# A list scheduler that ranks the operations that read PSUM first, in a two-layer hybrid mixer

## The chip, the cores and the metric

The kernel runs on one core of a Trainium2 chip. The core has a matrix engine (TensorE, PE in the rows; its weight loads are a row of their own, PEld), a vector engine (VectorE, DVE), a scalar engine (ScalarE, ACT), GpSimd (POOL) and a queue of transfers issued by SyncE (SP). TensorE writes its results into PSUM; VectorE and ScalarE read them there and put them into SBUF, which is called an eviction here. The metric is the time of the program on the device in microseconds (us).

## The reference

Two layers of a transformer-like mixer. Four token mixers share one input projection; each result is gated, projected up, merged under a sigmoid gate, and projected out. 512 latent tokens and 256 context tokens; the context stream is updated in the first layer only. All numbers are fp32.

```python
def reference(x, c, ctx, c_ctx, norm_gain, w_mod, b_mod, w_in, ...):
    xc = ctx
    for l in range(DEPTH):                       # 2 layers, D_MODEL 1024, 512 latent and 256 context tokens
        need_ctx = l < DEPTH - 1
        shift, scale, gate = jnp.split((silu_c @ w_mod[l] + b_mod[l])[:, None, :], 3, axis=-1)
        shift_c, scale_c, gate_c = jnp.split(silu_cc @ w_mod[l] + b_mod[l], 3)
        h = rmsnorm(x, norm_gain[l]) * (1.0 + scale) + shift
        hc = rmsnorm(xc, norm_gain[l]) * (1.0 + scale_c) + shift_c
        za, zb, zh, zf, zg = jnp.split(h @ w_in[l], SPLIT_IDX, axis=-1)      # 15 blocks of 256 columns
        zc = hc @ (w_in[l] if need_ctx else w_in[l][:, :SPLIT_IDX[2]])
        ya, yca = mixer_diff_attn(za, ...)       # softmax attention, differential, rotary
        yb, ycb = mixer_neigh_attn(zb, ...)      # windowed softmax attention with a bias
        yh, ych = mixer_hgrn2(zh, ...)           # gated linear recurrence, both directions
        yf = fourier_mix(zf)                     # 2-D DFT
        x = x + gate * merge_branches(h, (ya, yb, yh, yf), zg, w_up[l], w_merge[l], w_out[l])
        if need_ctx:
            xc = xc + gate_c * merge_branches(hc, (yca, ycb, ych, ycf), zc_parts[4], ...)
    return x

def merge_branches(h, ys, g, w_up_l, w_merge_l, w_out_l):
    gs = jnp.split(g, N_BRANCH, axis=-1)
    acc = None
    for i in range(N_BRANCH):
        branch = (ys[i] * jax.nn.silu(gs[i])) @ w_up_l[i]
        term = jax.nn.sigmoid(h @ w_merge_l[i]) * branch
        acc = term if acc is None else acc + term
    return acc @ w_out_l
```

## The kernel before

**How the work is tiled.** Every large product is done on tiles of 128 rows by 256 to 512 columns. To keep fp32 precision each factor is split into a high part and a rest, and each product is three matmuls: high by high, high by rest, rest by high. For the weights, blocks `wraw` of 128x1024 are fetched by SyncE's queue; ScalarE writes the high part `wh` and VectorE the rest `wl`, in halves of 128x512 (`split`, L488; class `Weights`, L492). There are two buffers for `wraw` and four each for `wh` and `wl`. For the activations the split pair is `h_hi` and `h_lo`.

**PSUM.** It is divided into three pools (L369 to L371): three buffers of 128x512 named `psg` for the large products and many small ones, one buffer `pst`, and two of 128x1024 named `psw`. A tile must be evicted before its buffer takes the next one. `psg` of the merge is read by a tanh on ScalarE into `mth` (`merge`, L1481); `psg` of a modulation or gate is made by `spread` (L617: eight products with a block of 32 columns, `psg<-u,cst`) and copied by ScalarE into `mrow` (`mod_rows`, L633).

**The layer boundary.** At the end of the first layer the output projection of each 128 tokens is multiplied by the gate on VectorE (`gu<-psg,u`), added to the stream (`u<-u,gu`), squared and summed. From the sums VectorE computes a reciprocal square root in a chain of small steps (`rsqrt`, L472; tiles `sm`), scales an identity matrix by it (`u<-kc,sm`), and TensorE multiplies the stream by that diagonal, which transposes and normalises it at once (`place`, L760; `psw<-u,u`). Two of the four 128x128 pieces of each such `psw` are evicted by ScalarE, two by VectorE (`u<-psw,modc`); then the result is split into `h_hi` and `h_lo`.

**What sets the order.** No instruction is issued where it is written. Each call is noted as an operation (`Program.record`, L199); neighbouring matmuls into one tile form one operation, which `mm3` (L580) cuts after every four products of three. Transfers are operations too. When all are known, `Program.order` (L255) builds the order that all engines follow: over and over it looks at the operations that are ready on each engine, computes from a table of costs when each could start (its producers' ends, its engine, a free buffer), and takes the one with the smallest pair of start time and rank (L289 and L303). Rank decides only between operations that could start at the same moment on one engine, or between engines. Rank is an operation's place in the program as written, less `ahead`: the fetches and splits of weights have `ahead` 400 (`AHEAD`, L165, set at L504 and L515), all others 0. Only operations up to 300 places beyond the oldest that isn't done are looked at (`WINDOW`, L286). `emit` then writes the instructions in this order, all at one line (L353), so that the rows of the profile are told apart by their tiles. On the chip each engine runs its own list strictly in that order.

**The stages.** In each layer the projections and the mixers are laid one over the other: first the Fourier, recurrence and differential-attention projections, then four merges (Fourier, recurrence, differential attention, neighbourhood attention), then the output projection and, after the first layer, the boundary. The first layer takes about 0 to 890 us, the second the rest.

Of the kernel before, what the change touches and what calls it, by code (L numbers as in the profile page):

```python
# [135 lines left out]
def _overlap(a, b):  # L136
    if a[0] >= b[1] or b[0] >= a[1]:
        return False
    return any(x0 < y1 and y0 < x1 for x0, x1 in a[2] for y0, y1 in b[2])


def _covers(a, b):
    return a[0] <= b[0] and a[1] >= b[1] and all(any(x0 <= y0 and y1 <= x1 for x0, x1 in a[2]) for y0, y1 in b[2])
# [20 lines left out]
WINDOW = 300  # L164
AHEAD = 400  # L165
BEHIND = 0
ATOM = 4
LAT = {"tensor": 0.2, "vector": 0.13, "scalar": 0.15, "gpsimd": 0.13}


class Program:
# [27 lines left out]
    def record(self, engine, method, args, kw):  # L199
        writes = [v for v in [args[0], kw.get("accum_out")] if isinstance(v, View)]  # L200
        reads = [v for v in list(args[1:]) + [v for k, v in kw.items() if k != "accum_out"] if isinstance(v, View)]
        dma = method == "dma_start"
        last = self.last
        if engine == "tensor" and last is not None and last.engine == "tensor" and last.tiles[0] is args[0].tile:
            op = last
        else:
            op = Op(len(self.ops), engine)
            op.rank -= self.ahead
            self.ops.append(op)
        self.last = op  # L210
        op.calls.append((engine, method, args, kw))
        for v in writes + reads:
            if v.tile not in op.tiles:
                op.tiles.append(v.tile)
                v.tile.touch += 1
        for v, w in [(v, False) for v in reads] + [(v, True) for v in writes]:
            r = v.region()
            log = v.tile.log
            for q, x, xw in log:
                if (w or xw) and x is not op and _overlap(r, q):  # L220
                    op.preds.add(x)
            if w:
                log[:] = [e for e in log if not _covers(r, e[0])]
            log.append((r, op, w))
        op.cost += self.price(engine, method, args, kw)
        op.latency = 2.0 if dma else LAT[engine]
        if dma:
            op.transfer = math.prod(args[0].shape) * 4 / 3e5
# [129 lines left out]
def tile_hybrid_mixers(ctx, tc, io, out, dump=None):  # L358
# [28 lines left out]
    def psg():  # L387
        return pg.tile([P, 512], F32, tag="g", name=nm("psg"))
# [7 lines left out]
    def act(out, in_, func=AF.Copy, **kw):  # L396
        nc.scalar.activation(out, in_, func, **kw)
# [181 lines left out]

    def mm3(ps, pairs, atom=ATOM):  # L580
        n = len(pairs)
        nc.ahead = -BEHIND
        for k, (sh, sl, mh, ml) in enumerate(pairs):
            if k % atom == 0:
                nc.cut()
            mm(ps, sh, mh, k == 0, False)
            mm(ps, sh, ml, False, False)
            mm(ps, sl, mh, False, k == n - 1)
        nc.ahead = 0

    def gemm_a(wh, wl, cs, n0, n1, ps=None, atom=ATOM):
        ps = (psg() if ps is None else ps)[:, 0:n1 - n0]
        mm3(ps, [(wh[k][:, cs], wl[k][:, cs], hi_t[:, k, n0:n1], lo_t[:, k, n0:n1]) for k in range(8)], atom)
        return ps
# [7 lines left out]
    def a_ranges(full):  # L602
        return ((0, 384), (384, 768)) if full else ((0, 512),)
# [594 lines left out]
    def hg_gates(l, j, z):  # L1198
# [4 lines left out]
        for d in range(2):  # L1203
            wide = psw() if first else None
            for i, (n0, n1) in enumerate(a_ranges(True)):
                ps = gemm_a(wh, wl, slice(P * d, P * (d + 1)), n0, n1, wide[:, 512 * i:512 * i + 512] if first else None, 2 if first else ATOM)
                nc.vector.tensor_scalar(z["f", j][d][:, n0:n1], ps, -1.0, 80.0, ALU.mult, ALU.min)
# [4 lines left out]
    def hg_query(l, z):  # L1212
        wh, wl = chunk()
        z["q"] = [slot() for _ in range(2)]
        for j in range(2):
            for n0, n1 in a_ranges(l == 0):
                ps = gemm_a(wh, wl, slice(P * j, P * (j + 1)), n0, n1, None, 2 if l == 0 else ATOM)
                act(z["q"][j][:, n0:n1], ps, AF.Copy, scale=0.5)
# [500 lines left out]
```

## Time and profile before

| what | value |
|---|---|
| time, median of 3 runs (lowest to highest) | 1495.21 us (1494.02 to 1495.75) |
| the profiled execution: its time | 1493.43 us |
| its span, first to last instruction | 1491.7 us |
| granted TensorE clock | 1.000 |
| TensorE busy | 1436.5 us (96%) |
| VectorE busy | 950.8 us (64%) |
| ScalarE busy | 627.6 us (42%) |
| GpSimd busy | 107.2 us (7%) |

The span is what the rows below are counted in; the profiled execution took 1.73 us more than it. In the rows, `psg<-u,cst` means that an instruction reads tiles `u` and `cst` and writes `psg`; what stands in square brackets is the time that the engine was idle just before and the producer whose signal ended it. A wait of TensorE is a loss of time when nothing later takes it up.

### The profile page before, as it was taken

The page shows a single profiled execution, that of the slowest core. Times are in us where ns is not written, and L with a number is a line of the kernel's source. Part 1 is how long each engine was busy: PE and PEld are TensorE (multiplying, and loading weights), DVE is VectorE, ACT ScalarE, POOL GpSimd, SP SyncE. Part 2 cuts the span into 40 slices and gives each one's busy share as a digit, 9 for nine tenths or more (in the row PEclk, how much of TensorE's full clock was granted, in tenths as well). Part 3 has the DMA queues.
Part 4 walks back from the last instruction along what each step waited for, and adds up shares of the span by engine and source line. Part 5 has one row for each costly group of instructions (what it writes and reads, how often), then busy time and mean ns, then how long its engine had stood idle before and what let it go on. Part 6 is the DMA issues. An engine that isn't in the chain of part 4 may idle for free.

```text
span 1491.7 us, 25385 instructions
## 1 busy us (share of the span) xinstructions
PE 1436.5 (96%) x10068; PEld 1317.4 (88%) x10068; DVE 950.8 (64%) x2058; ACT 627.6 (42%) x1384; POOL 107.2 (7%) x207
## 2 busy tenths in 40 slices
PE   1999999999999999999999999999999999999998
PEld 0899989999999999999999989898888889888788
DVE  5696898677663267633444477889867755674544
ACT  3444353465532245422323354535456633543330
POOL 0000000500000000100000110000130000110000
PEclk9999999999999999999999999999999999999999
DMA  9311101622321135543123321101353222464322
GB/s 349 103 44 57 33 30 60 138 70 97 107 89 57 57 82 169 140 132 123 57 78 101 96 98 57 57 33 58 90 143 88 89 74 88 141 160 160 104 96 78
DMA packets 50598, 144.76 MB, mean 97 GB/s; under 512 B 7280, under 2 KB 12400, under 8 KB 50480
## 3 DMA queue, kind: packets, MB, share of 16 engines
q1 hardware_dynamic: 38336, 112.21, 23.1%
q0 software_dynamic: 12144, 30.93, 8.4%
q8 instruction: 79, 1.29, 0.4%
q14 instruction: 39, 0.32, 0.1%
HBM read 123.98 MB, written 4.19 MB: 86 GB/s over the span
## 4 chain that ended last, share of the span: by engine, by line
PE 86%; DVE 5%; ACT 4%; issue 2%; DMA 2%; SPq 1%; POOL 0%; ACTq 0%; DVEq 0%; POOLq 0%
PE psg L353 70%; PE psw L353 11%; PE pst L353 5%; DVE u L353 4%; ACT u L353 3%; ACT wh L353 1%; DMA u<-u 1%; SPq L353 1%; DVE sm L353 1%; DMA u<-in_w_mod_dram 1%; ACT mth L353 0%; DVE wl L353 0%; DVE nss L353 0%; DVE dd L353 0%; DVE h_lo L353 0%
## 5 line engine op out<-in xcount | busy, mean ns | idle before, releaser
L353 PE MATMUL psg<-h_hi,wh 128*128 128x384 f32 (+2 forms) x1216 | 438.5, 361 | 2.9 <-ACT mth L353 2.8
L353 PE MATMUL psg<-h_hi,wl 128*128 128x384 f32 (+2 forms) x1216 | 428.6, 352 | 0.0
L353 PE MATMUL psg<-h_lo,wh 128*128 128x384 f32 (+2 forms) x1216 | 428.0, 352 | 0.3 <-DVE h_lo L353 0.3
L353 DVE TENSOR_TENSOR wl<-wraw,wh 128x512 fp32r<-128x512 f32 x312 | 201.6, 687 | 186.1 <-ACT wh L353 185.4
L353 ACT ACTIVATE wh<-wraw 128x512 fp32r<-128x512 f32 x312 | 180.6, 625 | 259.3 <-PE psg L353 246.5
L353 PEld LDWEIGHTS psg<-h_hi,wh 128*128 128x128 f32 x1216 | 228.7, 188 | 23.7 <-ACT mth L353 5.7
L353 PEld LDWEIGHTS psg<-h_hi,wl 128*128 128x128 f32 x1216 | 228.5, 188 | 16.0
L353 PEld LDWEIGHTS psg<-h_lo,wh 128*128 128x128 f32 x1216 | 228.9, 188 | 14.5 <-DVE h_lo L353 0.5
L353 PE MATMUL psg<-wh,h_hi 128*128 128x256 f32 x544 | 157.1, 289 | 0.0
L353 PE MATMUL psg<-wl,h_hi 128*128 128x256 f32 x544 | 151.6, 279 | 0.0
L353 PE MATMUL psg<-wh,h_lo 128*128 128x256 f32 x544 | 151.5, 279 | 0.0
L353 PE MATMUL psw<-u,u 64*128 64x128 f32 (+6 forms) x1144 | 135.4, 295 | 8.8 <-ACT u L353 3.1
L353 PEld LDWEIGHTS psw<-u,u 64*128 64x128 f32 (+2 forms) x1144 | 110.8, 188 | 22.0 <-issue 6.0
L353 ACT ACTIVATE u<-psw,sm 128x768 f32<-128x768 f32 (+2 forms) x120 | 90.7, 758 | 77.6 <-DVE sm L353 75.1
L353 DVE SCALAR_TENSOR_TENSOR mth<-mth,psg 128x384 f32<-128x384 f32 (+1 forms) x96 | 57.1, 594 | 87.3 <-ACT mth L353 72.9
L353 ACT ACTIVATE u<-psw 128x768 f32<-128x768 f32 (+10 forms) x208 | 93.8, 472 | 44.2 <-PE psw L353 40.9
L353 PE MATMUL psg<-wh,u 128*128 128x256 f32 x640 | 110.6, 277 | 0.9 <-ACT mth L353 0.9
L353 ACT ACTIVATE mth<-psg 128x384 f32<-128x384 f32 (+1 forms) x120 | 62.3, 520 | 113.2 <-PE psg L353 112.9
L353 PE MATMUL psg<-yg,wh 128*128 128x384 f32 (+1 forms) x384 | 107.1, 360 | 0.0
L353 PEld LDWEIGHTS psg<-wh,h_hi 128*128 128x128 f32 x544 | 102.2, 188 | 3.8
L353 PEld LDWEIGHTS psg<-wl,h_hi 128*128 128x128 f32 x544 | 103.0, 189 | 0.2
L353 PEld LDWEIGHTS psg<-wh,h_lo 128*128 128x128 f32 x544 | 102.3, 188 | 0.0
(134 smaller groups left out, 1960.1 us busy)
## 6 DMA issues: line engine op xcount, KB each, us to landing
wraw<-in_w_merge_dram SPq DMA_DIRECT2D x64, 512.0 KB, 3.5
wraw<-in_w_in_dram SPq DMA_DIRECT2D x60, 512.0 KB, 3.8
u<-in_w_mod_dram SPq DMA_DIRECT2D x32, 384.0 KB, 6.4
wraw<-in_w_up_dram SPq DMA_DIRECT2D x16, 512.0 KB, 3.5
wraw<-in_w_out_dram SPq DMA_DIRECT2D x16, 512.0 KB, 3.8
u<-u POOLq DMA_DIRECT2D x72, 96.0 KB, 2.4
u<-in_w_gate_dram SPq DMA_DIRECT2D x16, 384.0 KB, 6.3
u<-u POOLq DMA_DIRECT2D x24, 192.0 KB, 2.8
```

The costliest lines, as they stand in the source:

```text
L353: getattr(getattr(nc, engine), method)(*map(f, args), **{k: f(v) for k, v in kw.items()})
```

## The change

The rank of an operation of VectorE or ScalarE (or GpSimd) that reads a PSUM tile is its place less 500, where it was its place. Splits and fetches of weights keep their 400. So of two operations that could start at the same moment on VectorE or ScalarE, an eviction up to 100 places later in the program than a weight split is taken before it, and one up to 500 places later than any other operation is taken before that. No operation is added or taken away (4,837 before and after), and buffers and costs are the same.

```diff
@@ -164,6 +164,7 @@
 WINDOW = 300
 AHEAD = 400
 BEHIND = 0
+EVICT = 500
 ATOM = 4
 LAT = {"tensor": 0.2, "vector": 0.13, "scalar": 0.15, "gpsimd": 0.13}
 
@@ -200,12 +201,13 @@
         writes = [v for v in [args[0], kw.get("accum_out")] if isinstance(v, View)]
         reads = [v for v in list(args[1:]) + [v for k, v in kw.items() if k != "accum_out"] if isinstance(v, View)]
         dma = method == "dma_start"
+        evict = not dma and engine != "tensor" and any(v.tile.space == "ps" for v in reads)
         last = self.last
         if engine == "tensor" and last is not None and last.engine == "tensor" and last.tiles[0] is args[0].tile:
             op = last
         else:
             op = Op(len(self.ops), engine)
-            op.rank -= self.ahead
+            op.rank -= EVICT if evict else self.ahead
             self.ops.append(op)
         self.last = op
         op.calls.append((engine, method, args, kw))
```

How it moves instructions, at three places. In the names of these rows the first number is the tile's, the second a running number of the instruction that wrote it; the emitting line is L353 before and L355 after.

The first is ScalarE's list where the first of the modulations of the first layer's merges stands, around 438 us: `psg_857` is the product of `spread`, `mrow_858` its copy, the `mth` are tanh evictions, `wh_859` and `wh_868` the high parts of weights in two halves. Before:

```order
L353 ACTIVATE mth_840_4717<-psg_839_4620 128x384
L353 ACTIVATE mth_847_4754<-psg_846_4689 128x384
L353 ACTIVATE wh_868_4788<-wraw_854_4592 128x512 x2
L353 ACTIVATE mth_852_4793<-psg_851_4740 128x384
L353 ACTIVATE mrow_858_4796<-psg_857_4779 128x256
L353 ACTIVATE mth_862_4847<-psg_861_4798 128x384
```

After:

```order
L355 ACTIVATE mth_840_4711<-psg_839_4629 128x384
L355 ACTIVATE wh_859_4714<-wraw_842_4574 128x512 x2
L355 ACTIVATE mth_847_4743<-psg_846_4645 128x384
L355 ACTIVATE mth_852_4788<-psg_851_4745 128x384
L355 ACTIVATE wh_868_4790<-wraw_854_4626 128x512 x2
L355 ACTIVATE mrow_858_4809<-psg_857_4779 128x256
L355 ACTIVATE mth_862_4847<-psg_861_4793 128x384
```

The two halves of `wh_868` stood ahead of `mth_852`, and stand behind it now. The other thirteen places of this kind have the same change.

The second is VectorE's list at the layer boundary: `sm_1514` to `sm_1517` are the last steps of a reciprocal square root, `u_1518` the diagonal that TensorE's next `psw` needs, `wl_1561` and `wl_1566` weight splits, `gu_1531` an eviction, `u_1484` the sum with it. Before:

```order
L353 SCALAR_TENSOR_TENSOR sm_1514_9141<-sm_1514_9141,sm_1511_9131 128x2
L353 TENSOR_TENSOR u_1484_8320<-u_1484_8320,gu_1528_9152 128x256
L353 SCALAR_TENSOR_TENSOR sm_1517_9194<-sm_1514_9141,sm_1516_9184 128x2
L353 TENSOR_TENSOR h_lo_74<-u_1524_9161,h_hi_73 128x4x128
L353 TENSOR_SCALAR u_1518_9211<-kc_91,sm_1517_9194 128x128 x2
L353 TENSOR_TENSOR h_lo_74<-u_1526_9180,h_hi_73 128x4x128
L353 TENSOR_TENSOR wl_1561_9218<-wraw_1492_8940,wh_1560_9209 128x512 x2
L353 TENSOR_TENSOR wl_1566_9234<-wraw_1509_8980,wh_1565_9225 128x512 x2
L353 TENSOR_TENSOR gu_1531_9245<-psg_1530_9166,u_1401_7205 128x256
L353 TENSOR_SCALAR u_1542_9238<-psw_1541_9220,modc_855_7399 128x128
L353 TENSOR_TENSOR u_1484_8320<-u_1484_8320,gu_1531_9245 128x256
```

After:

```order
L355 TENSOR_TENSOR u_1484_8326<-u_1484_8326,gu_1528_9151 128x256
L355 TENSOR_TENSOR sm_1514_9142<-sm_1516_9190 128x2
L355 TENSOR_TENSOR h_lo_74<-u_1526_9182,h_hi_73 128x4x128
L355 TENSOR_TENSOR wl_1561_9210<-wraw_1492_8940,wh_1560_9205 128x512
L355 TENSOR_TENSOR gu_1531_9214<-psg_1530_9167,u_1401_7203 128x256
L355 TENSOR_TENSOR wl_1561_9210<-wraw_1492_8940,wh_1560_9205 128x512
L355 TENSOR_TENSOR wl_1566_9220<-wraw_1509_8980,wh_1565_9216 128x512 x2
L355 SCALAR_TENSOR_TENSOR sm_1514_9142<-sm_1514_9142,sm_1511_9133 128x2
L355 TENSOR_TENSOR u_1484_8326<-u_1484_8326,gu_1531_9214 128x256
L355 SCALAR_TENSOR_TENSOR sm_1517_9229<-sm_1514_9142,sm_1516_9190 128x2
L355 TENSOR_SCALAR u_1518_9233<-kc_91,sm_1517_9229 128x128 x2
```

One split of activations (`h_lo` of `u_1526`), four halves of weight splits, the eviction `gu_1531` and its sum into `u_1484` stood behind `u_1518`; the last steps of the chain, from the second `sm_1514` to `u_1518`, stand behind all of them but for that sum's place just ahead of `sm_1517`.

The third is TensorE's list where the first attention of layer 0 begins its products, around 95 us: `psg_180` is a projection's tile, `psw_144`, `psw_145` and `psw_148` are products on attention's rotated tiles `u_139` and `u_140`. Before:

```order
L353 MATMUL psg_180_804<-wl_152_684,h_hi_73 128x256
L353 MATMUL psg_180_804<-wh_151_660,h_lo_74 128x256
L353 MATMUL psw_148_857<-u_140_839,u_127_732 128x128 x6
L353 MATMUL psw_144_867<-u_131_686,u_139_855 128x128 x6
L353 MATMUL psg_186_823<-wh_151_660,h_hi_73 128x256
L353 MATMUL psg_186_823<-wl_152_684,h_hi_73 128x256
```

After:

```order
L355 MATMUL psg_186_825<-wh_134_599,h_lo_74 128x256
L355 MATMUL psw_144_845<-u_131_680,u_139_820 128x128 x6
L355 MATMUL psw_145_852<-u_131_680,u_139_820 128x128 x6
L355 MATMUL psg_180_806<-wh_151_654,h_hi_73 128x256
L355 MATMUL psg_180_806<-wl_152_678,h_hi_73 128x256
L355 MATMUL psg_180_806<-wh_151_654,h_lo_74 128x256
```

`psw_144` stood behind twelve matmuls of `psg_180` and behind `psw_148`, `psw_145` further down; both stand ahead of the twelve now.

## Rows read from the trace of the kernel before

**Rows 1.** Page: busy time with share and instructions; a group: busy, mean ns, idle before
```profile
PE 1436.5 (96%) x10068; PEld 1317.4 (88%) x10068; DVE 950.8 (64%) x2058; ACT 627.6 (42%) x1384; POOL 107.2 (7%) x207
...
L353 PE MATMUL psg<-h_hi,wl 128*128 128x384 f32 (+2 forms) x1216 | 428.6, 352 | 0.0
```

**Rows 2.** What TensorE waited for: us in total, times, longest us
```profile
PE psw L353 <- DVE u L353: 10.5, 8, 6.8
PE psg L353 <- ACT mth L353: 6.6, 14, 0.5
PE psw L353 <- ACT u L353: 5.4, 9, 1.1
...
PE psg L353 <- ACT sm L353: 1.1, 1, 1.1
```

**Rows 3.** The same for weight loads (PEld)
```profile
PEld psg L353 <- ACT mth L353: 13.8, 15, 1.0
```

**Rows 4.** Timeline around 438: start us, us, engine line operation count [idle before <-releaser]
```profile
437.41 1.15 ACT L353 ACTIVATE wh<-wraw 128x512 fp32r<-128x512 f32 x2 [4.54 <-PE psg L353]
...
437.48 1.07 PE L353 MATMUL psg<-u,cst 128*32 128x256 f32 x16
...
438.47 0.47 ACT L353 ACTIVATE mth<-psg 128x384 f32<-128x384 f32 x1
...
438.99 0.19 PEld L353 LDWEIGHTS psg<-h_hi,wh 128*128 128x128 f32 x1 [0.92 <-ACT mth L353]
438.99 0.44 PE L353 MATMUL psg<-h_hi,wh 128*128 128x384 f32 x1 [0.44 <-ACT mth L353]
```

**Rows 5.** Timeline around 621, another spread without a split ahead
```profile
621.33 0.52 PEld L353 LDWEIGHTS psg<-kc,mrow 128*128 128x128 f32 x4 [0.41 <-ACT mth L353]
621.33 0.61 PE L353 MATMUL psg<-kc,mrow 128*128 128x2 f32 x4
```

**Rows 6.** Timeline around 885, the layer boundary
```profile
883.50 1.14 ACT L353 ACTIVATE wh<-wraw 128x512 fp32r<-128x512 f32 x2
883.84 0.49 DVE L353 TENSOR_SCALAR u<-kc,sm 128x128 f32<-128x128 f32 x2
884.23 0.70 DVE L353 TENSOR_TENSOR h_lo<-u,h_hi 128x512 fp32r<-128x512 f32 x1
...
884.28 2.02 PE L353 MATMUL psw<-u,u 128*128 128x128 f32 x16 [0.90 <-DVE u L353]
...
884.83 2.51 DVE L353 TENSOR_TENSOR wl<-wraw,wh 128x512 fp32r<-128x512 f32 x4
...
885.97 1.49 ACT L353 ACTIVATE u<-psw,modc 128x128 f32<-128x128 f32 x4
...
887.24 0.44 DVE L353 TENSOR_TENSOR gu<-psg,u 128x256 f32<-128x256 f32 x1
...
887.89 0.44 DVE L353 TENSOR_TENSOR u<-u,gu 128x256 f32<-128x256 f32 x1
...
888.75 1.02 PE L353 MATMUL psw<-u,u 128*128 128x128 f32 x7 [2.44 <-issue]
```

**Rows 7.** Timeline around 142, and a row at 966
```profile
141.15 1.15 ACT L353 ACTIVATE wh<-wraw 128x512 fp32r<-128x512 f32 x2 [3.17 <-PE psg L353]
...
142.73 0.38 PE L353 MATMUL psg<-u,u 128*128 128x1 f32 x2 [1.10 <-ACT sm L353]
...
965.88 0.76 PE L353 MATMUL psw<-kc,u 128*128 128x128 f32 x5 [0.38 <-ACT u L353]
```

**Rows 8.** Timeline around 95, two matmul starts and a wait
```profile
94.26 0.28 PE L353 MATMUL psg<-wh,h_hi 128*128 128x256 f32 x1
...
94.49 0.28 PE L353 MATMUL psg<-wh,h_lo 128*128 128x256 f32 x1
...
96.00 1.80 PE L353 MATMUL psw<-u,u 64*128 64x128 f32 x24 [0.88 <-DVE u L353]
```

**Rows 9.** Windows, attention of layer 1: us, busy (instructions) per engine, granted clock, DMA
```profile
1040.00:1269.00 229.00, 228.80 (x1433) 197.07 (x1431) 162.60 (x369) 111.61 (x232) 27.09 (x55) 1.00 0.33 94
```

## The prediction

> **What bounds the kernel now.** I read the page first. TensorE is busy 1436.5 us, 96% of the span; VectorE and ScalarE have 36% and 58% of the span free [rows 1]. So the time is TensorE's work plus its waits, 55 us in a span of 1491.7, and an order of the other engines can only be worth what it does to those waits. The list of TensorE's waits comes next. Four rows are in reach of evictions: waits for VectorE at `psw` (10.5 us, of which one, early, has 6.8), for ScalarE's tanh at `psg` (6.6 us in 14 waits, none over 0.5), for ScalarE at `psw` (5.4 in nine) and one of 1.1 us at small products [rows 2]. That bounds a gain: those four rows together are 23.6 us, less the 6.8 in the opening, whose order hardly changes, so at most 17. Fourteen of these waits are the same event, which the timeline shows [rows 4].
>
> **First part: the tanh ahead of the weight splits.** At 437.41 ScalarE takes two halves of `wh` (1.15 us), although the tanh that frees a `psg` is ready when TensorE begins `spread` at 437.48. The tanh comes at 438.47, takes 0.47, and TensorE, which finished `spread` by 438.55, goes on at 438.99, idle 0.44 [rows 4]. Once the tanh stands first, it would end about 0.6 us after 437.48, at 438.1, half a microsecond before `spread` is through. The whole wait goes, and the copy to `mrow`, which follows the tanh or the split, is needed only by a later product. By TensorE's own row 14 such waits are 6.6 us [rows 2]. By the weight loads they are 13.8 in 15 [rows 3], from which what passes between two such products without any wait has to come off: 0.41 where the tanh was not late and TensorE's row shows no idle at all [rows 5]; 13.8 - 15 x 0.41 = 7.6. I take the middle, -7.1, and -6.6 to -7.6 as its range.
>
> [...]
>
> What the splits cost when they come 0.5 us later: nothing, as long as the weights are early. The 1216 matmuls that read `wl` directly in front of a projection never waited, 0.0 us [rows 1]. If that cover were gone, a split half would cost its own 0.57 us of ScalarE (half of 1.15) at each place.
>
> **Second part: the layer boundary.** Here the change loses. TensorE's next `psw` needs the diagonal `u<-kc,sm`, which VectorE begins at 883.84; TensorE waits 0.90 for it and starts at 884.28. After that it waits 2.44 at 888.75; the row names no producer, and I read it as a `psw` buffer, whose evictions on VectorE stand behind four `wl` halves (2.51) and `gu` [rows 6]. In the new order the four `wl`, one `h_lo`, `gu` and its sum stand ahead of the end of the chain. That is 2.51 + 0.70 + 0.44 + 0.44 = 4.1 us of VectorE's work [rows 6] that the diagonal now waits for, and TensorE has nothing else to do there. It is up to 5.2 if a `wl` must also wait for its pair of `wh` (1.14). Back comes a part of the 2.44: the evictions no longer stand behind splits, and what remains is about half of ScalarE's four evictions (1.49), 0.8, so up to 1.6 is given back, or nothing if these evictions are late for another reason. The term is between 4.1 - 1.6 = 2.5 and 5.2. I take +4.0, near the middle, since neither the extra wait nor the full return has a row that decides it.
>
> **Third part: smaller waits that go.** At 142 two `wh` halves (1.15) run ahead of the evictions that TensorE needs; it waits 1.10 [rows 7]. With those evictions first, ScalarE starts them where it started the splits, and some 0.8 of the 1.10 goes. Of the nine waits for ScalarE at `psw`, 5.4 us in all or 0.6 each [rows 2], I find one that stands behind such a pair, 0.38 at 966 [rows 7]. The sum is -1.2; 0 if other evictions queue in front, -2.7 if two or three more of the nine go, at 0.6.
>
> **Fourth part: matmuls brought ahead of their producers.** An eviction that comes earlier in the planned order brings forward the products that read it, and TensorE takes them in the list's order whether they are ready or not. At 96 TensorE already waits 0.88 for VectorE's rotated tile [rows 8]. Now `psw_144` and `psw_145` stand ahead of twelve matmuls of a projection, which start 0.115 us apart (two steps from 94.26 to 94.49). So TensorE arrives 12 x 0.115 = 1.4 us earlier and waits longer by as much, less what VectorE brings that tile forward; I book 0.9. For the rest, in the recurrence of layer 1 and the attention, I book 0.4. Ends: 0, and 4 if three places lose 1.4 each. The term is +1.3.
>
> **Sum.** -7.1 + 4.0 - 1.2 + 1.3 = -3.0. The profiled execution took 1493.43 us (span 1491.7 and 1.73 around it), so 1490.4; it lay 1.78 below the median of 1495.21, which makes the forecast 1492.2. With each term at a likely end, its own range is 1489.5 to 1495.
>
> **Rivals.** *The evictions pay in full.* The boundary loses only 2.5, three more short waits go, nothing is brought forward too far: -7.6 + 2.5 - 2.7 = -7.8, 1487.4 us. For it speaks that each wait in [rows 2] is one for an eviction; against it, that only two places outside the fourteen show a split in front.
>
> *The wait moves to the weights.* If the splits' delay of 0.57 us shows at half of the places and more, half of the first term comes back: -7.1 turns into -3.6, the sum into +0.5, the time 1495.7, no change. Against it speaks the 0.0 of the matmuls that read `wl` [rows 1]; for it, that ScalarE is often filled without a gap after such an event, as the splits follow right behind the tanh.
>
> *Slower, by the attention of layer 1.* From 1040 to 1269 TensorE is busy 228.80 of 229.00 us [rows 9]: there is nothing to gain, and only here is the order so tight that everything brought forward can lose. The mechanism is that of 96: a score or a transposed tile stands in TensorE's list ahead of projection matmuls, and TensorE waits 0.88 + 1.4 = 2.3 [rows 8] for VectorE with those matmuls behind it. One such place doesn't decide; three (6.9 us) turn -3.0 into +3.9; with four, 9.2 less the 1.3 already booked, the time is 1500.1. Against it: VectorE and ScalarE are free for 29% and 51% of this stretch.
>
> *The fourteen waits stay.* If TensorE waited for want of `psg` buffers and not for the tanh's turn, a new order would not help: 4.0 - 1.2 + 1.3 = +4.1, 1499.3. Against it: a hand-over without a split in front shows no idle [rows 5]. [...]
>
> **How the numbers follow.** Forecast 0.42, evictions in full 0.25, wait moves 0.16, slower by the attention 0.13, waits stay 0.04. About 0.2%, 3.0 us, is what a measurement of this kernel can tell from no change, so faster is below 1492.2, slower above 1498.2. The forecast lies on that bound and is split 0.21 and 0.21: faster 0.46, same 0.37, slower 0.17. The range reaches from below the first rival, 1485.5, to 1499.5, just short of the attention rival.
>
> **What would show it.** Right: the row of TensorE's waits for the tanh at `psg` disappears; a wait for VectorE at `psw` near 884 grows from 0.9 to about 5 and the one near 889 shrinks; the wait near 142 falls to some 0.3; that near 96 grows to about 1.8; TensorE's busy time stays at 1436 us. Wrong: waits at `psw` or `pst` between 1040 and 1269, matmuls that wait for `wh` or `wl`, the fourteen waits still there, or no growth at 884.

## The result and the profile after

The changed kernel takes 1486.97 us (median of 5 runs, 1486.55 to 1487.79), the kernel before, in the same series, 1494.02 (1493.24 to 1495.75): ratio 0.995, 95% interval 0.9938 to 0.9961. It is faster by 7 us, where 3.0 were forecast; the range held it, and the time is that of the first rival, though it did not come about in that rival's way. The profiled execution has a span of 1485.2 us, 6.5 less than before.

The busy time on the page of the changed kernel, and what TensorE and its weight loads waited for (us in total, times, longest):

```profile
PE 1434.3 (97%) x10068; PEld 1318.6 (89%) x10068; DVE 948.1 (64%) x2058; ACT 627.6 (42%) x1384; POOL 106.9 (7%) x207
```

```profile
PE psw L355 <- DVE u L355: 12.0, 7, 7.6
PE psw L355 <- ACT sq L355: 6.3, 1, 6.3
PE psw L355 <- ACT u L355: 3.5, 7, 0.8
...
PE psg L355 <- ACT sm L355: 0.2, 1, 0.2
```

```profile
PEld psg L355 <- ACT mth L355: 5.8, 14, 0.4
```

The row of TensorE waiting for the tanh [rows 2] is gone, and the weight loads' 13.8 us [rows 3] are 5.8, which is the 0.41 of a hand-over without a wait, fourteen times. The fifteenth of before was such a hand-over too [rows 5], so by the weight loads the tanh cost 13.8 less 0.4 less 5.8, 7.6 us; by TensorE's row, in which the wait at 438.99 reads 0.44 where the weight loads' reads 0.92 [rows 4], it cost 6.6. In place of these waits stands one of 6.3 us at `psw`. TensorE's busy time is 2.2 us less than before [rows 1].

The first of the fourteen places, to be read against [rows 4]:

```profile
434.92 1.07 PE L355 MATMUL psg<-u,cst 128*32 128x256 f32 x16
435.02 0.49 ACT L355 ACTIVATE mth<-psg 128x384 f32<-128x384 f32 x1 [5.75 <-PE psg L355]
435.41 1.15 ACT L355 ACTIVATE wh<-wraw 128x512 fp32r<-128x512 f32 x2
...
435.92 0.19 PEld L355 LDWEIGHTS psg<-h_hi,wh 128*128 128x128 f32 x1 [0.41 <-ACT mth L355]
435.92 0.45 PE L355 MATMUL psg<-h_hi,wh 128*128 128x384 f32 x1
```

The tanh now begins 0.10 us after `spread`, the splits follow it, and TensorE goes on without idle time in its own row. The next is the layer boundary, where [rows 6] was:

```profile
872.90 0.41 DVE L355 TENSOR_SCALAR u<-psw,modc 128x128 f32<-128x128 f32 x1 [0.53 <-ACT u L355]
...
874.83 0.41 DVE L355 TENSOR_SCALAR u<-psw,modc 128x128 f32<-128x128 f32 x1 [0.53 <-ACT u L355]
...
876.24 0.15 DVE L355 TENSOR_TENSOR sm<-sm 128x2 f32<-128x2 f32 x1
...
876.43 0.69 DVE L355 TENSOR_TENSOR h_lo<-u,h_hi 128x512 fp32r<-128x512 f32 x1
877.04 0.68 DVE L355 TENSOR_TENSOR wl<-wraw,wh 128x512 fp32r<-128x512 f32 x1
...
877.64 0.42 DVE L355 TENSOR_TENSOR gu<-psg,u 128x256 f32<-128x256 f32 x1
...
877.97 1.88 DVE L355 TENSOR_TENSOR wl<-wraw,wh 128x512 fp32r<-128x512 f32 x3
...
879.78 0.15 DVE L355 SCALAR_TENSOR_TENSOR sm<-sm,sm 128x2 f32<-128x2 f32 x1
879.85 0.41 DVE L355 TENSOR_TENSOR u<-u,gu 128x256 f32<-128x256 f32 x1
880.18 0.15 DVE L355 SCALAR_TENSOR_TENSOR sm<-sm,sm 128x2 f32<-128x2 f32 x1
...
880.37 0.48 DVE L355 TENSOR_SCALAR u<-kc,sm 128x128 f32<-128x128 f32 x2
...
880.80 6.97 PE L355 MATMUL psw<-u,u 128*128 128x128 f32 x32 [6.28 <-ACT sq L355]
...
887.53 0.42 PE L355 MATMUL psg<-h_hi,wh 128*128 128x384 f32 x1
```

From 876.24 to 880.37 VectorE does one `h_lo`, four `wl`, `gu` and the sum between two steps of the chain; then come the diagonal and TensorE, after 6.28 us idle. The row names a square on ScalarE as releaser; what TensorE multiplies by is the diagonal, begun at 880.37. By windows (us, busy of PE, PEld, DVE, ACT and POOL with instructions, granted clock, DMA share, GB/s):

```profile
880.80:884.70 3.90, 3.80 (x17) 3.51 (x17) 2.24 (x14) 0.98 (x4) 0.00 (x0) 0.50 0.59 215
884.70:887.50 2.80, 2.80 (x16) 2.80 (x17) 1.69 (x6) 1.83 (x4) 0.00 (x0) 0.61 0.00 0
887.50:892.00 4.50, 4.50 (x34) 4.48 (x33) 3.63 (x13) 3.17 (x7) 0.00 (x0) 1.00 0.02 4
```

Behind the wait the granted clock is 0.50 until about 887; the 0.61 of the second window is a mean over the step back to 1.00. Before, it was 1.00 there, as two windows of the kernel before show:

```profile
884.00:889.00 5.00, 2.27 (x18) 2.14 (x19) 5.00 (x13) 4.10 (x13) 0.98 (x2) 1.00 0.74 216
889.00:894.00 5.00, 5.00 (x36) 5.00 (x36) 4.93 (x22) 3.80 (x8) 0.00 (x0) 1.00 0.38 147
```

Both kernels hold the same operations, so each matmul can be found in both traces; the lead is how much earlier it starts in the changed kernel. The lead is 2.6 us ahead of the first of the eleven spreads of layer 0 that had a wait, and 8.7 behind the last, of which 5.9 come at the eleven places themselves; at the boundary the lead falls from 8.9 to 3.0; at the end it is 6.5.

### The profile page after: what moved, and what is told of

It reads as the page before. It is cut to its first block, busy times and chain, and to the rows that moved or that the text cites. A ratio compares the mean times of both kernels' runs of the same rounds, so it can differ in the third digit from the quotient of the medians.

```text
span 1485.2 us, 25324 instructions
## 1 busy us (share of the span) xinstructions
PE 1434.3 (97%) x10068; PEld 1318.6 (89%) x10068; DVE 948.1 (64%) x2058; ACT 627.6 (42%) x1384; POOL 106.9 (7%) x207
## 4 chain that ended last, share of the span: by engine, by line
PE 89%; DVE 6%; ACT 3%; SPq 1%; issue 1%; DMA 1%; ACTq 0%; DVEq 0%
PE psg L355 72%; PE psw L355 12%; PE pst L355 5%; DVE u L355 4%; ACT u L355 3%; SPq L355 1%; DVE sm L355 1%; DMA u<-in_w_mod_dram 1%; DVE wl L355 1%; DVE nss L355 0%; DVE h_lo L355 0%; ACT h_hi L355 0%; DVE dd L355 0%; ACT wh L355 0%; DVE gu L355 0%
## 5 line engine op out<-in xcount | busy, mean ns | idle before, releaser
L355 PE MATMUL psg<-h_hi,wh 128*128 128x384 f32 (+2 forms) x1216 | 438.6, 361 | 0.5 <-ACT h_hi L355 0.5
L355 PE MATMUL psg<-h_hi,wl 128*128 128x384 f32 (+2 forms) x1216 | 428.7, 353 | 0.0
L355 PE MATMUL psg<-h_lo,wh 128*128 128x384 f32 (+2 forms) x1216 | 428.1, 352 | 0.3 <-DVE h_lo L355 0.3
L355 DVE TENSOR_TENSOR wl<-wraw,wh 128x512 fp32r<-128x512 f32 x312 | 204.0, 684 | 99.0 <-ACT wh L355 98.8
L355 PEld LDWEIGHTS psg<-h_hi,wh 128*128 128x128 f32 x1216 | 228.7, 188 | 20.1 <-ACT mth L355 2.5
L355 PEld LDWEIGHTS psg<-h_hi,wl 128*128 128x128 f32 x1216 | 228.5, 188 | 16.0
L355 PEld LDWEIGHTS psg<-h_lo,wh 128*128 128x128 f32 x1216 | 228.9, 188 | 14.6 <-DVE h_lo L355 0.5
L355 ACT ACTIVATE wh<-wraw 128x512 fp32r<-128x512 f32 x312 | 181.3, 624 | 79.4 <-PE psg L355 74.7
L355 ACT ACTIVATE mth<-psg 128x384 f32<-128x384 f32 (+1 forms) x120 | 63.2, 527 | 247.7 <-PE psg L355 239.5
L355 DVE SCALAR_TENSOR_TENSOR mth<-mth,psg 128x384 f32<-128x384 f32 (+1 forms) x96 | 57.2, 596 | 168.2 <-ACT mth L355 151.7
L355 PE MATMUL psg<-wh,h_hi 128*128 128x256 f32 x544 | 156.3, 287 | 0.0
L355 PE MATMUL psg<-wl,h_hi 128*128 128x256 f32 x544 | 151.6, 279 | 0.0
L355 PE MATMUL psg<-wh,h_lo 128*128 128x256 f32 x544 | 151.5, 279 | 0.0
L355 PE MATMUL psw<-u,u 64*128 64x128 f32 (+6 forms) x1144 | 137.5, 297 | 11.0 <-ACT sq L355 6.3
L355 PEld LDWEIGHTS psw<-u,u 64*128 64x128 f32 (+2 forms) x1144 | 112.7, 192 | 22.8 <-issue 11.8
L355 ACT ACTIVATE u<-psw,sm 128x768 f32<-128x768 f32 (+2 forms) x120 | 90.6, 758 | 77.5 <-DVE sm L355 73.6
L355 ACT ACTIVATE u<-psw 128x768 f32<-128x768 f32 (+10 forms) x208 | 93.7, 472 | 60.7 <-PE psw L355 46.5
L355 PE MATMUL psg<-wh,u 128*128 128x256 f32 x640 | 110.7, 277 | 0.0
L355 PE MATMUL psg<-yg,wh 128*128 128x384 f32 (+1 forms) x384 | 106.5, 359 | 0.0
L355 PEld LDWEIGHTS psg<-wh,h_hi 128*128 128x128 f32 x544 | 102.4, 188 | 3.3
L355 PEld LDWEIGHTS psg<-wl,h_hi 128*128 128x128 f32 x544 | 102.9, 189 | 0.1
L355 PEld LDWEIGHTS psg<-wh,h_lo 128*128 128x128 f32 x544 | 102.3, 188 | 0.0
```

The lines of the kernel that those rows point to most:

```text
L355: getattr(getattr(nc, engine), method)(*map(f, args), **{k: f(v) for k, v in kw.items()})
```

## The experiments

All are compared with the kernel before on the chip that they ran on, whose median differed by up to 3.4 us between chips; so ratios are compared between series. A span is that of one execution, often the fastest of its series, and spans of one kernel in one series differ by 1 to 4 us; a gain that is read from spans alone is no surer than that.

| kernel | ratio to the kernel before | 95% interval | span of the profiled execution, us |
|---|---|---|---|
| full change | 0.9950 | 0.9938 to 0.9961 | 1485.2 |
| after_again (the same) | 0.9940 | 0.9927 to 0.9954 | 1484.1 |
| tanh_only | 0.9909 | 0.9896 to 0.9923 | 1481.5 |
| tanh_again (the same) | 0.9915 | 0.9901 to 0.9928 | 1481.2 |
| act_only | 0.9956 | 0.9944 to 0.9968 | 1488.7 |
| dve_only | 1.0015 | 1.0007 to 1.0024 | 1497.8 |
| chain_first | 0.9931 | 0.9919 to 0.9944 | 1483.2 |
| no_boundary | 0.9926 | 0.9912 to 0.9939 | 1479.6 |
| boundary_only | 1.0023 | 1.0013 to 1.0033 | 1495.7 |
| busy | 0.9947 | 0.9935 to 0.9960 | 1483.6 |
| e350 | 1.0013 | 1.0004 to 1.0022 | 1494.0 |
| ahead20 | 1.0019 | 1.0011 to 1.0028 | 1498.1 |
| nb_fill | 0.9896 | 0.9880 to 0.9913 | 1478.2 |

**tanh_only: the tanh evictions alone.**

```diff
-evict = not dma and engine != "tensor" and any(v.tile.space == "ps" for v in reads)
+evict = engine == "scalar" and args[0].tile.tag == "mth" and any(v.tile.space == "ps" for v in reads)
```

> Only ScalarE's tanh evictions into mth get the first rank; all other evictions keep their old rank. Theory (the tanh ahead of the splits pays by itself, and the loss at the layer boundary comes from other evictions): the 14 waits at psg go, weight loads wait for the tanh 5.8 us instead of 13.8, so -8.0 us; the boundary keeps its two waits of 0.90 and 2.44; 1494.0 - 8.0 = 1486.0. Rival (the gain lies mostly in the mixers' small evictions, as -6.5 and a boundary loss of the same size might suggest): 1491 or more.

The span is 10.2 us below that of before, and 3.7 below that of the full change. The weight loads wait 5.8 us for the tanh, and the boundary keeps its two waits, as the theory said:

```profile
877.51 2.02 PE L355 MATMUL psw<-u,u 128*128 128x128 f32 x16 [0.91 <-DVE u L355]
...
881.96 2.02 PE L355 MATMUL psw<-u,u 128*128 128x128 f32 x16 [2.43 <-issue]
```

The fourteen places give 7.6 us of it. The other 2.6 were not expected: most of them are three later waits of the kernel before, of 0.59, 0.62 and 0.91 us near 600, 1269 and 1323, that are gone. Why was not looked into. One rule for one kind of eviction does more than the whole change. Both were run again on one chip:

> The changed kernel unaltered, on the same chip as the next two. Theory: ratio 0.995 as at first, the wait of 6.3 us at the boundary. Rival: none; it is the yardstick.

> The kernel with only the tanh evictions first, again, beside the full change on one chip. Theory (the rest of the full change costs more than it brings): span 1481.5, 3.7 us below the full change; ratio 0.992. Rival (its 0.991 came from a chip on which the kernel before was slow): no difference from the full change, ratio 0.995.

On one chip they are at 1484.37 and 1487.38 us; the intervals of the ratios only just touch (0.9928 and 0.9927), the spans differ by 2.9, the first time by 3.7. The rest of the full change costs some 3 us.

**act_only and dve_only: one engine's evictions.**

```diff
-evict = not dma and engine != "tensor" and any(...)
+evict = engine == "scalar" and not dma and any(...)     # act_only; "vector" in dve_only
```

> Only evictions on ScalarE get the first rank. VectorE's list keeps the reciprocal square root's end and the diagonal ahead of the weight splits at the layer boundary. Theory: the 14 waits go (-8.0), the boundary stays at 0.90 + 2.44, and of some 5 us that the full change gained in the mixers at least half comes from ScalarE (-2.5): 1494.0 - 10.5 = 1483.5. Rival (the boundary is lost by ScalarE's evictions going first): a wait of about 6.3 us at the boundary and 1488 to 1490.

> Only evictions on VectorE get the first rank. Theory: the 14 waits for the tanh stay (13.8 us on weight loads), the boundary has a wait of about 6.3 us and a lower granted clock behind it (+6.5), the mixers gain up to 2.5: 1494.0 + 6.5 - 2.5 = 1498. Rival (the boundary's loss needs both engines' evictions moved): 1491.5 to 1494.

dve_only is much as expected: the tanh waits stay, and the boundary waits 5.10 us (6.3 expected). So it is VectorE's evictions that cost the boundary. act_only misses: its ratio is 0.9956, where 1483.5 of 1494.0 would be 0.993, some 4 us. At the boundary it waits about as before (0.49 and 3.05 us), but in the mixers of layer 0 the lead turns from 0.6 ahead at 212 us to 6.2 behind at 314. From 290 to 320, in the differential attention, TensorE is busy 26.23 of 30 us at a clock of 0.89; before, 28.84 at 1.00 (the two windows, act_only first):

```profile
290.00:320.00 30.00, 26.23 (x171) 22.99 (x169) 19.13 (x43) 17.16 (x38) 7.14 (x15) 0.89 0.38 87
```

```profile
290.00:320.00 30.00, 28.84 (x210) 26.62 (x209) 22.23 (x47) 18.67 (x41) 6.39 (x13) 1.00 0.29 60
```

The full change has 28.84 and 1.00 there. Which of VectorE's evictions saves it was not looked into.

**boundary_only and no_boundary: the one place.**

```diff
+evict = self.evict and not dma and engine != "tensor" and any(...)    # in record
 ...
+nc.evict = full          # boundary_only: on here, off elsewhere; no_boundary: `not full`, on elsewhere
 norm = Norm(mc)
 ...
 for x in pend:
     norm.place(*x)
+nc.evict = False         # no_boundary: True
```

> Evictions get the first rank only while the output projection and the boundary of the first layer are recorded; all else as before. Theory: the boundary's wait of 5 to 6.3 us with the lower clock behind it, nothing else: span 1491.7 + 6.5 = 1498.2, ratio 1.0044. Rival (the lost time is taken up by later waits): 1492 to 1494.

> The full change, but while the output projection and the boundary of the first layer are recorded no eviction gets the first rank. VectorE's list there is that of the kernel before. Theory (the boundary is the one place where the change loses, 6.5 us): span 1485.2 - 6.5 = 1478.7, granted clock 1.00 at the boundary, 8.4 to 9 us ahead of the kernel before on both sides of it; ratio 0.991. Rival (what is won at the boundary is given back at the next waits of layer 1): 1482 to 1485, ratio 0.995.

boundary_only waits 6.27 us and falls about 6 behind; later waits take up 2, so that 4.0 remain. This is between theory and rival. no_boundary has the span 1479.6, 5.6 below the full change, where the theory asked for 6.5; by its ratio, 0.9926 beside 0.9950 and 0.9940, it is 2 to 4 us below, between theory and rival. In its trace the two waits are those of before, but the matmuls behind the second are slow, 3.61 us where they took 2.02, which is more than the 0.9 that are missing:

```profile
875.56 2.02 PE L356 MATMUL psw<-u,u 128*128 128x128 f32 x16 [0.92 <-DVE u L356]
...
880.01 3.61 PE L356 MATMUL psw<-u,u 128*128 128x128 f32 x16 [2.42 <-issue]
```

```profile
881.00:884.00 3.00, 3.00 (x17) 3.00 (x17) 2.32 (x9) 1.43 (x4) 0.00 (x0) 0.61 0.45 172
```

**chain_first: the chain ahead of all.**

```diff
 m = t1 - t0
+nc.ahead = 600
 r = self.rstd(t0, t1, n)
 ...
+nc.ahead = 0
 return dg
```

> The full change, and the steps of the reciprocal square root and the diagonal at the layer boundary get a rank of 600 less than their place, ahead of evictions and splits. Theory: the wait of 6.28 us at the boundary shrinks to about 1, the granted clock stays at 1.00 there, and the time is 1487.0 - 6.5 = 1480.5. Rival (what TensorE waits for at the boundary is the psw evictions or the stream's sum, which the chain's rank doesn't move): 1486 to 1487.

The wait of 6.28 becomes 1.04, so the chain was what TensorE waited for. But two others follow, 2.21 for an eviction and 1.79 for `h_lo`, which the chain now overtakes:

```profile
876.80 2.02 PE L355 MATMUL psw<-u,u 128*128 128x128 f32 x16 [1.04 <-ACT h_hi L355]
...
881.03 3.24 PE L355 MATMUL psw<-u,u 128*128 128x128 f32 x16 [2.21 <-DVE u L355]
...
886.38 0.44 PE L355 MATMUL psg<-h_lo,wh 128*128 128x384 f32 x1 [1.79 <-DVE h_lo L355]
```

The span is 1483.2, 2.0 below the full change, but the interval of the ratio (0.9919 to 0.9944) overlaps those of the full change: of the 6.5 us hoped for, two came at most. The time is that of the rival, for another reason. Here a rank moved the wait about.

**busy and nb_fill: what the lower clock costs.** Both add products that nothing reads, the one where the full change waits 6.28, the other where no_boundary waits 2.42. The code is that of nb_fill; busy reads two columns in its first product and gives the products a rank of 100 more.

```diff
+def fill(z):
+    nc.cut()
+    ps = pst()
+    mm(ps[:, 0:P], ident, z)          # waits for the diagonal (nb_fill), or for a late step of the chain (busy)
+    for k in range(FILL):             # 7 in nb_fill, 18 in busy
+        mm(ps[:, P:2 * P], ident, ident, k == 0, k == FILL - 1)
+    nc.cut()
```

> The full change, and 18 products of the identity with itself into the free pst buffer, which nothing reads, put where TensorE waits at the boundary (they begin when a late step of the reciprocal square root is there). No other instruction moves. Theory (about half of the 6.5 us is the lower granted clock behind the wait: 32 matmuls that take 6.97 us, where 16 took 2.02 at 1.00): the wait in TensorE's row shrinks to under 2, the clock stays at 1.00 and the 32 matmuls take 4.0 to 5 us; span 1485.2 - 2 to 3 = 1482.7. Rival (those matmuls are slow because psw buffers are evicted slowly): clock 1.00 but span 1485.

> As no_boundary, and eight products with the identity into the free pst buffer, which nothing reads, between the two groups of psw at the boundary, where TensorE waits 2.42 us. Theory (after the same two waits the granted clock fell in no_boundary and not in tanh_only, and the 16 matmuls behind took 3.61 us, not 2.02): with TensorE busy there the clock stays at 1.00, the 16 take 2.0, span 1479.6 - 1.6 = 1478.0. Rival (the clock fell for another reason, or its price is hidden as in busy): the 16 take 3.6 again, or the span stays at 1479.6.

In busy the filling works, and the clock stays at 1.00, but at the boundary nothing is won:

```profile
877.30 4.26 PE L356 MATMUL pst<-kc 128*128 128x128 f32 x36
...
881.83 2.02 PE L356 MATMUL psw<-u,u 128*128 128x128 f32 x16 [0.26 <-ACT sq L356]
...
884.76 1.16 PE L356 MATMUL psw<-u,u 128*128 128x128 f32 x8 [0.91 <-ACT u L356]
...
887.87 1.16 PE L356 MATMUL psw<-u,u 128*128 128x128 f32 x8 [0.44 <-ACT u L356]
...
888.78 0.42 PE L356 MATMUL psg<-h_hi,wh 128*128 128x384 f32 x1
```

From the first `psw` to the first projection it is 6.95 us (881.83 to 888.78), with the lower clock it was 6.73 (880.80 to 887.53). TensorE now waits for the evictions instead, 0.91 and 0.44 in these rows. The rival held: the ratio is that of the full change. The expectation is wrong in one point: behind the products other instructions did move, some of VectorE's and a few of TensorE's, and the span, 1.6 below the full change, holds that too. The second trace of the unaltered kernel, after_again, shows the same from the other side. There the clock was back at 1.00 sooner behind the same wait, and TensorE waited for evictions; the stretch is 6.27 us (881.13 to 887.40):

```profile
881.13 3.41 PE L355 MATMUL psw<-u,u 128*128 128x128 f32 x16 [6.27 <-ACT sq L355]
884.98 1.16 PE L355 MATMUL psw<-u,u 128*128 128x128 f32 x8 [0.44 <-ACT u L355]
...
887.40 0.42 PE L355 MATMUL psg<-h_hi,wh 128*128 128x384 f32 x1
```

```profile
884.70:887.50 2.80, 2.17 (x17) 1.98 (x18) 2.04 (x7) 2.25 (x6) 0.00 (x0) 1.00 0.00 0
```

In the trace of nb_fill the same means shortens the stretch:

```profile
875.72 2.02 PE L357 MATMUL psw<-u,u 128*128 128x128 f32 x16 [0.86 <-DVE u L357]
...
877.81 1.73 PE L357 MATMUL pst<-kc 128*128 128x128 f32 x14
...
880.14 2.02 PE L357 MATMUL psw<-u,u 128*128 128x128 f32 x16 [0.60 <-issue]
```

The 16 matmuls take 2.02, not 3.61, and the span is 1.4 less (1.6 expected). Here, it seems, the buffers are free when TensorE comes, so that its own speed decides. That time is won is not shown: the other three runs of nb_fill have spans of 1479.6 to 1480.2, the five of no_boundary 1479.6 to 1481.9, and among these one with a mean granted clock of 1.000 has 1479.9. The ratio is the lowest of all, though its interval overlaps those of no_boundary and tanh_only.

**e350 and ahead20: other numbers.**

```diff
-EVICT = 500        # e350, in the changed kernel
+EVICT = 350
-AHEAD = 400        # ahead20, in the kernel before
+AHEAD = 20
```

> EVICT is 350, not 500: evictions go ahead of other operations up to 350 places earlier, but a weight split (400) still goes ahead of an eviction of about the same place. Theory: the 14 waits for the tanh are back (weight loads 13.8 us), the boundary still loses its 6.5 us, since there the chain's steps and not splits are overtaken, and the mixers gain as with 500: span 1485.2 + 8.0 = 1493.2. Rival (what is overtaken doesn't matter, only that evictions come early): 1485 to 1487.

> The kernel before with AHEAD = 20 instead of 400 and no rule for evictions: fetches and splits of weights keep a lead of 20 places. Theory (what counts is that a split doesn't go ahead of the tanh and of the boundary's evictions, whichever rank says so): the 14 waits go (-8.0), the 2.44 at the boundary shrinks to about 1 (-1.4), span 1491.7 - 9.4 = 1482.3. Rival (the lead of 400 is what keeps the weights early): matmuls wait for wh or wl, some 0.6 us at many of the 156 blocks, span above 1492.

e350 came out as the theory said (1494.0; 6.3 us of waits for the tanh, 6.3 at the boundary). As no operation over 300 places beyond the oldest is looked at, 350 and 500 differ only against the splits. So the fourteen places hang on evictions against splits, the boundary on evictions against the chain. ahead20 showed neither of its cases; its span is that of the rival, but no matmul waits for `wh` or `wl` in TensorE's row. The tanh waits went, the second wait at the boundary shrank to 1.32, but TensorE waits for VectorE where the recurrence of layer 0 and that of layer 1 begin. I put that down to splits that are done later and fill VectorE there; no run separates it:

```profile
100.86 3.90 PE L353 MATMUL psw<-u,u 64*128 64x128 f32 x36 [2.38 <-DVE u L353]
```

```profile
932.01 1.38 PE L353 MATMUL psw<-u,u 64*128 64x128 f32 x16 [3.91 <-DVE u L353]
```

## Why the prediction was right, and where its sum was not

**What bounds the kernel.** Right for the first two terms: the change is worth what it does to TensorE's waits. Ahead of the first spread the gain is in no wait, as the third and fourth terms show.

**First term, -7.1.** It is -7.6: eleven spreads of layer 0 give 5.9 us of lead, three of layer 1 give 1.7. The weight loads' rows had said 7.6, TensorE's own 6.6; the weight loads were right.

**Second term, +4.0, between 2.5 and 5.2.** The sign and the place were right, the size was not: the lead falls by 5.9 (8.9 to 3.0). The wait grew by 5.4, from 0.90 to 6.28. Of these, the work that the forecast added up to 4.1 makes 3.7 by starts (876.43 to 879.78, and 879.85 to 880.18); 1.7 more come from ahead of that, in part where VectorE's evictions, now first, stand between the earlier steps and wait for ScalarE's in turn (0.53 each at 872.90 and 874.83). The step that failed is the 1.6 to be given back. The wait of 2.44 is gone, but the four `psw` tiles take 6.73 us from first start to the next projection (6.27 in after_again), and took 6.25 before, from 884.28 [rows 6] to this row:

```profile
890.53 0.42 PE L353 MATMUL psg<-h_hi,wh 128*128 128x384 f32 x1
```

Splits or not, the evictions set the pace: among the four `psw` TensorE waits for them 0.44 us in after_again and up to 0.91 in busy. The two engines take turns, as these rows of the changed kernel show:

```profile
882.89 0.46 ACT L355 ACTIVATE u<-psw,modc 128x128 f32<-128x128 f32 x1 [2.09 <-PE psw L355]
883.38 0.73 DVE L355 TENSOR_SCALAR u<-psw,modc 128x128 f32<-128x128 f32 x2 [1.42 <-ACT u L355]
...
884.15 0.46 ACT L355 ACTIVATE u<-psw,modc 128x128 f32<-128x128 f32 x1 [0.80 <-DVE u L355]
```

VectorE begins at 883.38, where ScalarE's 0.46 ends at 883.35, and ScalarE again at 884.15, where VectorE's 0.73 ends at 884.11; each is idle, 1.42 and 0.80 us, until the other's eviction releases it. In the whole traces of both kernels 169 tiles of PSUM are read by both engines, and never at one time. Two engines evicting one tile are not twice as fast here.

**Third and fourth terms, -1.2 and +1.3.** Together they are about -4.8 (7.6 and 4.8 gained, 5.9 lost, 6.5 in all), where +0.1 was forecast. The wait at 142 fell from 1.10 [rows 7] to 0.2, as forecast. At 96 I had TensorE arrive too early and wait 0.9 longer. (The products there are those of the recurrence, not of an attention as the words ahead of that order say; the argument is the same.) `psw_144` and `psw_145` start at 92.90 without a wait, because what brought them forward had brought their tiles forward too; a wait as long as before [rows 8] comes at the next products, near 100. But what the term feared does happen once, at 183, where the recurrence's second pass begins and TensorE did not wait before; dve_only has that wait as well (1.42):

```profile
100.03 1.32 PE L355 MATMUL psw<-u,u 64*128 64x128 f32 x14 [0.85 <-DVE u L355]
...
182.90 1.61 PE L355 MATMUL psw<-u,u 64*128 64x128 f32 x24 [1.67 <-DVE u L355]
```

So the waits do not explain the lead of 2.6 ahead of the first spread. Up to it TensorE is idle for 36.2 us before and for 36.3 after; what is shorter is its busy time, 401.28 and 398.62 (the kernel before first):

```profile
0.00:437.48 437.48, 401.28 (x3032) 377.40 (x3032) 323.38 (x726) 207.11 (x467) 31.72 (x67) 1.00 0.32 99
```

```profile
0.00:434.92 434.92, 398.62 (x3033) 375.58 (x3033) 323.65 (x726) 207.07 (x466) 31.71 (x67) 1.00 0.32 100
```

The same matmuls in another order take 2.7 us less; the cause stays open. The rest, some 2.2 us, lies behind: 0.4 between the spreads of layer 0 and 1.8 in layer 1, where tanh_only gains 1.7 without any other eviction moved. There the waits for ScalarE at `psw` are shorter; of the 1.9 us by which their row fell (5.4 in nine to 3.5 in seven) 1.4 lie in layer 1.

That the time fell well inside the range is in part luck: the first term gave 0.5 more than booked, the boundary lost 1.9 more, and the third and fourth gave 4.9 more, over half of it by something that the forecast had not named.

**The rivals.** The wait did not move to the weights. The attention of layer 1 stayed without a wait, to be read against [rows 9]:

```profile
1040.00:1269.00 229.00, 228.71 (x1423) 196.69 (x1422) 159.98 (x356) 113.14 (x233) 29.34 (x60) 1.00 0.34 97
```

The fourteen waits did not stay, so it was not too few buffers that made them, but the order of those who free them. "The evictions pay in full" has the right time by the wrong way: its boundary was to lose 2.5 and lost 5.9, and its short waits were to give 2.7, where 4.8 came, over half of it not from waits.

## What to carry to other kernels

A rank for a whole class of operations is many changes at once: here one member of the class brought more than the class (tanh_only 0.991, full change 0.995), and one place took back about half of what the others gave (5.9 of 12.4 us). Look for the place where the favoured engine is the bound, and there for the short chain that everything waits for. Where a wait repeats with one length, compare it with the same hand-over without the rival instruction: here the difference was the gain, 7.6 us in fourteen places.

## What the runs showed of the hardware that was not expected

The granted clock did not follow from the length of a wait alone. tanh_only and no_boundary both waited 0.9 and 2.4 us at the boundary with the same 16 matmuls between; in the one the clock stayed at 1.00 and the next 16 took 2.02, in the other it fell (0.61 over three us) and they took 3.61. What sets the two apart was not found, and it need not be the kernel: behind the same wait the clock of the full change was 0.61 from 884.70 to 887.50 in its first trace and 1.00 in its second. In act_only (0.89 from 290 to 320) it was 0.84 from 290 to 300, where no wait was longer than 1.19 us. With eight unread products in the second wait it stayed at 1.00 (nb_fill, 870 to 887), and with eighteen in the long one as well (busy, 874.50 to 887.80). But the slow clock did not always cost time: in busy, where it did not fall, the stretch was no shorter (6.95 us, and 6.73 with the slow clock).
